# Preparing the value products of a hybrid decoder block: scale roots spread earlier, the first tile loaded whole, twelve warm-up matmuls

## The chip, the cores and the metric

The kernel runs on one core of a Trainium2 chip. The metric is the device time of one execution, in microseconds (us). TensorE (PE) multiplies, VectorE (DVE) and ScalarE (ACT) do the elementwise work, GpSimd (POOL) here only takes powers, and SyncE (SP) issues the transfers between the chip's memory and the on-chip buffers, one after another from one queue.

## The reference, cut to what matters

```
xn = rmsnorm(x, norm1_g)                         # x: 1024 tokens x 1024 channels
qa, ka, va, qr, kr, vr, gr, gate_a, gate_b = pieces of xn @ w_in
qa, ka = per-head rmsnorm
o_a = three groups of dilated sliding-window attention, mixed by their denominators
o_r = retention(qr, kr, vr), per-head groupnorm, times silu(gr)
y = sigmoid(gate_a) * (o_a @ w_proj_a) + sigmoid(gate_b) * (o_r @ w_proj_b)
x = x + y @ w_out
x = x + square(relu(rmsnorm(x, norm2_g) @ w_up)) @ w_down
```

All tensors are float32. The change touches only the first stage: the norm of `x` and `va`, the 1024 x 1536 values of attention, three column blocks of 512.

## The kernel before, in words

**Splits.** Each operand of a product is kept as two tensors, a rounded one (`xh`, `wh`, written by ScalarE) and the rest (`xl`, `wl`, by VectorE); `split` writes both (lines 401 and 404). A product is three matmuls for each 128 channels, xh.wh, xh.wl, xl.wh (line 297).

**Weights.** `W` streams the weights: `load` issues a transfer on SP, `pump` works through a list of steps (splits, and additions of weight quarters, line 157) as far as `W.limit` lets it, `hold` bounds the loads. `request(n)` raises `hold`, `weight_sums(n)` raises `limit`.

**The values.** The 1024 tokens are 8 tiles of 128. Column block 0 is done plainly: `columns(t)`, 24 matmuls. Blocks 1 and 2 for all tokens are done as a 2 x 2 block product with seven instead of eight products: N1 (`first_part`) and N2 (`second_part`) for tiles 0 to 3, 12 matmuls each, then N6, N5, N7, N3, N4, four tiles of 12 each, whose operands are sums of pieces of the normalised input (`sums`, line 734, then `put_sum`, which splits them). `keep_part`, `add_parts` and `keep_columns` move results out of the accumulators and `store` them.

**The norm.** `x` arrives twice: transposed (`load_k(t)`, operand layout) and in rows (`load_x(t)`). `root(t)` squares and sums the rows on ScalarE, takes the power on GpSimd, and writes a diagonal matrix of the roots on VectorE (line 634). `spread(t)` is a matmul of ones with that diagonal (line 646), which lays the roots along the free dimension. `times_root(t)` multiplies by them on VectorE, for a tile in `FUSED` by the norm weights at the same time (eight instructions, line 658), else in two instructions (line 661) after `times_g(t)` has done the norm weights on ScalarE (eight instructions, line 639). `put(t)` splits the result into the operand `X`. Tiles 0 and 1 (`RAWS`) are first multiplied without their roots (`raw_split`, lines 623 and 624), and the root is applied to the results.

**Order.** A call of a part emits its matmuls as one slot; `with_spread(t, fn)` puts a spread inside the slot of `fn`, behind half of a part's matmuls, or behind 9 of 24 in `columns`. In this stage ScalarE and VectorE run the instructions of the listed calls in the order in which they are emitted; work emitted outside the two `manual_schedule` blocks (the split of the weights of N5 and later, for instance) is placed among them by the scheduler of the framework, and so are SP's transfers. Matmuls of ones on a scratch operand (line 683) run ahead of the first product.

Of the kernel before, what the change touches and what calls it, by code (L numbers as in the profile page):

```python
# [19 lines left out]
D = 1024  # L20
# [17 lines left out]
class Weights:  # L38
# [10 lines left out]
    A, B, C, D = (0, 1), (2, 3), 5, 4  # L49
# [298 lines left out]
def hybrid_block(ctx: ExitStack, tc: tile.TileContext, a: dict, out: bass.AP):  # L348
    nc = tc.nc
# [76 lines left out]
    W = Weights(nc, rawp, wp, split)  # L426
# [165 lines left out]
    px = pool(first, "px", 2, "right")  # L592

    RAWS = 2
    FUSED = (2, 3, 0)
    ones = maskT[:, 0]
    busy = XS[0, 1][0][:, 0]
    col = gng.rearrange("p a b -> p (a b)")[:, :3 * NT].rearrange("p (t c) -> p t c", c=3)
# [4 lines left out]
    parts = [tuple(x[t // 2][:, t % 2 * 512:t % 2 * 512 + 512] for x in (half_a, half_e)) for t in range(4)]  # L603
    xk, xts = {}, {}

    def load_k(t, cut=slice(0, D)):

        to = half_e[t % 6] if t in (0, 1, 6) else px.tile([P, D], F, name="xk")
        xk[t] = to.rearrange("p (k t) -> p k t", k=KT)
        nc.sync.dma_start(to[:, cut], a["x_t"][t][:, cut])  # L610

    def load_x(t):
        xts[t] = px.tile([P, D], F, name="xt") if t else half_a[1]
        nc.sync.dma_start(xts[t], a["x"][t * P:(t + 1) * P, :])
# [14 lines left out]
    def root(t):  # L629

        nc.scalar.activation(xts[t], xts[t], AF.Square, accum_out=col[:, t, 0:1])
        rsqrt(col[:, t, 1:2], col[:, t, 0:1], 1.0 / D)
        dg[t] = FX[1, t // 4][:, 3, t % 4 * P:t % 4 * P + P]
        nc.vector.tensor_scalar(dg[t], ident, col[:, t, 1:2], None, op0=OP.mult)

    def times_g(t, ks=range(KT)):

        for k in ks:
            nc.scalar.activation(xk[t][:, k], xk[t][:, k], AF.Copy, scale=gT[:, k:k + 1])
# [11 lines left out]
    def times_root(t):  # L651

        pt = roots[t]
        for j in range(2):
            to = rooted(t, j)
            if t in FUSED:
                for k in range(4):
                    nc.vector.scalar_tensor_tensor(to[:, k], xk[t][:, 4 * j + k], gT[:, 4 * j + k:4 * j + k + 1],
                                                   pt[:, 0], op0=OP.mult, op1=OP.mult)
            else:  # L660
                nc.vector.tensor_tensor(to, xk[t][:, 4 * j:4 * j + 4], pt[:, 0:1].to_broadcast([P, 4, P]),
                                        op=OP.mult)

    def put(t):

        for j in range(2):
            split(*X(slice(4 * j, 4 * j + 4), tokens_of(t)), rooted(t, j))

    lo, hi = halves()
    with tc.manual_schedule(engines={mybir.EngineType.DVE, mybir.EngineType.Activation}):  # L670
        nc.sync.dma_start(gT, a["norm1_g"])
        load_k(0, slice(0, 512))
        W.limit = W.hold = 8
        W.load()
        load_k(0, slice(512, D))
        for _ in range(5):
            W.load()
        nc.vector.memset(busy.bitcast(F), 1.0)
        nc.vector.memset(ones, 1.0)
        nc.scalar.activation(col[:, 0, 2:3], half[:, 0:1], AF.Square)  # L680
        warm = mm.tile([P, 512], F, name="mm")
        for _ in range(9):
            nc.tensor.matmul(warm, busy[:, :P], busy, start=True, stop=True)
        raw_split(0, range(4))
        W.pump(1)
        raw_split(0, range(4, 6))
        W.pump(1)
        raw_split(0, range(6, 8))
        for _ in range(6):
            W.pump(1)  # L690
        load_k(1)
        load_x(0)
        nc.sync.dma_start(ident, a["c_ident"])
        load_k(2)
        load_x(2)
        load_x(1)
        load_k(3)
        raw_split(1, range(8))
# [29 lines left out]
    def sums(h, names):  # L728

        cut = slice(256 * h, 256 * h + 256)  # L730
        for name in names:
            t, u, op = {"N5": ((0, 0), (0, 1), OP.subtract), "N7": ((0, 1), (1, 1), OP.subtract),
                        "N6": ((1, 1), (0, 0), OP.add), "N4": ((1, 0), (1, 1), OP.subtract)}[name]
            nc.vector.tensor_tensor(FX[t][:, :, cut], FX[t][:, :, cut], FX[u][:, :, cut], op=op)

    def put_sum(name, h):

        cut = slice(256 * h, 256 * h + 256)
        split(*(x[:, :, cut] for x in operands[name]), FX[sums_of[name]][:, :, cut])
# [3 lines left out]

    nc.sync.dma_start(gqk[:, 0], a["q_norm_g"])
    nc.sync.dma_start(gqk[:, 1], a["k_norm_g"])
    SUM = {16: ("N5", 0), 17: ("N5", 1), 18: ("N7", 0), 19: ("N7", 1), 28: ("N4", 0), 29: ("N4", 1)}
    us, plain = W.take(4), W.take(4)
    made = {}
    raw = [t < RAWS for t in range(NT)]
# [1 line left out]
    def first_part(t):  # L751
        made["N1", t] = unit_part("N1", t, us[:2], ms, "ms")

    def second_part(t):
        made["N2", t] = unit_part("N2", t, us[2:], mm, "mm")

    def columns(t):
        made["P", t] = values(plain, tokens_of(t), t == NT - 1, ms, "ms")

    def keep_part(t):  # L760
        nc.scalar.activation(parts[t][0], made.pop(("N1", t)), AF.Copy, **({"scale": col[:, t, 1:2]} if raw[t] else {}))

    def add_parts(t):

        pm, vt = made.pop(("N2", t)), vp.tile([P, 512], F, name="vt")
        if raw[t]:
            nc.vector.scalar_tensor_tensor(vt, pm, col[:, t, 1:2], parts[t][0], op0=OP.mult, op1=OP.add)
        else:
            nc.vector.tensor_tensor(vt, pm, parts[t][0], op=OP.add)
        store(1, t, vt)  # L770

    def keep_columns(t):

        vt = vp.tile([P, 512], F, name="vt")
        nc.scalar.activation(vt, made.pop(("P", t)), AF.Copy, **({"scale": col[:, t, 1:2]} if raw[t] else {}))
        store(0, t, vt)

    def weight_sums(n):
        W.limit += n
        W.pump()  # L780

    def request(n):

        W.hold += n
        while W.load():
            pass

    def with_spread(t, fn):
        pipe.at(0, lambda: spread(t), lambda: None)
        fn()  # L790

    def open_sums():

        first.close()
        for name in ("N6", "N5"):
            open_slot(name)

    def save():
        for i, x in enumerate(XS[0, 1]):
            nc.sync.dma_start(xs_d[i], x.bitcast(F).rearrange("p a b -> p (a b)"))  # L800

    with tc.manual_schedule(engines={mybir.EngineType.DVE, mybir.EngineType.Activation}):
        first_part(0)
        second_part(0)
        columns(0)

        first_part(1)
        root(0)

        second_part(1)  # L810
        root(2)
        load_x(3)
        keep_part(0)
        add_parts(0)
        keep_columns(0)

        with_spread(2, lambda: columns(1))
        times_root(2)
        root(1)
        put(2)  # L820
        load_k(4)
        load_x(4)
        keep_part(1)
        add_parts(1)
        request(3)

        first_part(2)
        keep_columns(1)
        root(3)
        load_x(5)  # L830

        with_spread(3, lambda: second_part(2))
        times_root(3)
        load_k(5)
        times_g(4)

        with_spread(0, lambda: columns(2))
        keep_part(2)
        put(3)
        add_parts(2)  # L840
        times_root(0)
        load_k(6)
        root(4)
        load_x(6)
        put(0)
        weight_sums(2)
        request(3)

        with_spread(4, lambda: first_part(3))
        keep_columns(2)  # L850
        times_root(4)
        load_k(7)
        root(5)
        load_x(7)
        times_g(1, range(4))

        second_part(3)
        put(4)
        times_g(1, range(4, 8))
        weight_sums(1)  # L860

        with_spread(1, lambda: columns(3))
        keep_part(3)
        add_parts(3)
        times_root(1)
        put(1)
        weight_sums(2)
        times_g(5)
        root(6)

        with_spread(5, lambda: columns(4))
        keep_columns(3)
        times_root(5)
        put(5)
        weight_sums(1)
        times_g(6)
        sums(0, ("N5",))

        with_spread(6, lambda: columns(5))
        keep_columns(4)  # L880
        times_root(6)
        put(6)
        root(7)
        sums(0, ("N7", "N6"))
        times_g(7)

        with_spread(7, lambda: columns(6))
        keep_columns(5)
        times_root(7)
        put(7)  # L890
        open_sums()
        put_sum("N6", 0)
        weight_sums(2)

        columns(7)
        keep_columns(6)
        save()
        sums(1, ("N5", "N7", "N6"))
        put_sum("N6", 1)

    W.limit, W.hold = None, 18
    nc.vector.tensor_scalar(gqk[:, 0], gqk[:, 0], -DH ** -0.5, None, op0=OP.mult)
# [1 line left out]
    def front_step():  # L904
# [10 lines left out]
        if p == 28:  # L915
# [5 lines left out]
            open_slot("N4")  # L921
        if p in SUM:
            put_sum(*SUM[p])

# [183 lines left out]
    with ExitStack() as ph:  # L1108
# [6 lines left out]
        sums, squares = {}, {}  # L1115
# [281 lines left out]
    with ExitStack() as ph:  # L1397
# [115 lines left out]
        for i, (j, name) in enumerate(order):  # L1513
# [8 lines left out]
            if (j, name) in free:  # L1522
                u = free[j, name]
                lo, _ = halves()
# [121 lines left out]
    with ExitStack() as ph:  # L1646
# [56 lines left out]
        sums = {}  # L1703
# [126 lines left out]
    with ExitStack() as ph:  # L1830
# [5 lines left out]
        for u in range(1, len(units)):  # L1836
# [3 lines left out]
            c, t = units[u]  # L1840
# [112 lines left out]
```

## Time and profile before

| | us |
|---|---|
| median of 3 runs | 2156.54 (2155.95 to 2158.1) |
| the profiled execution, its time | 2162.37 |
| its span, first to last instruction | 2160.6 |
| first product (tile 0) starts | 6.41 |
| `first_part(1)` starts | 21.63 |
| `columns(7)` starts | 73.04 |
| N5 starts | 92.43 |

The profile shows one execution. TensorE is recorded busy 99% of the span; a matmul's record overlaps the next one's, so the distance of two starts tells more than a duration. The granted clock is the share of TensorE's full clock, 1.00 or less. In rows of the timeline the bracket names how long the engine had been idle, and who released it.

### The profile page before, as it was taken

The page shows a single profiled execution, that of the slowest core. Times are in us where ns is not written, and L with a number is a line of the kernel's source. Part 1 is how long each engine was busy: PE and PEld are TensorE (multiplying, and loading weights), DVE is VectorE, ACT ScalarE, POOL GpSimd, SP SyncE. Part 2 cuts the span into 40 slices and gives each one's busy share as a digit, 9 for nine tenths or more (in the row PEclk, how much of TensorE's full clock was granted, in tenths as well). Part 3 has the DMA queues.
Part 4 walks back from the last instruction along what each step waited for, and adds up shares of the span by engine and source line. Part 5 has one row for each costly group of instructions (what it writes and reads, how often), then busy time and mean ns, then how long its engine had stood idle before and what let it go on. Part 6 is the DMA issues. An engine that isn't in the chain of part 4 may idle for free.

```text
span 2160.6 us, 28517 instructions
## 1 busy us (share of the span) xinstructions
PE 2137.2 (99%) x9837; PEld 1751.6 (81%) x9837; DVE 1383.6 (64%) x2370; ACT 1110.5 (51%) x2125; POOL 311.1 (14%) x340
## 2 busy tenths in 40 slices
PE   9999999999999999999999999999999999999999
PEld 7787777788888888888888877778788888788887
DVE  6944434655556565657767776783865556788884
ACT  6625555434655454445545654542655555755552
POOL 0000000000000000003123110000000000777773
PEclk9999999999999999999999999999999999999999
DMA  8433333243667666665354587874254556745443
GB/s 317 153 106 113 103 96 114 99 138 132 189 202 217 205 197 195 214 182 168 107 173 129 160 288 237 273 235 147 87 161 143 160 156 195 237 157 186 161 141 108
DMA packets 296481, 366.15 MB, mean 169 GB/s; under 512 B 35136, under 2 KB 202496, under 8 KB 296080
## 3 DMA queue, kind: packets, MB, share of 16 engines
q1 hardware_dynamic: 295792, 364.06, 53.4%
q8 instruction: 77, 1.26, 0.2%
q14 instruction: 68, 0.56, 0.1%
q10 hardware_dynamic: 544, 0.26, 0.0%
HBM read 247.67 MB, written 116.59 MB: 169 GB/s over the span
## 4 chain that ended last, share of the span: by engine, by line
PE 81%; DVE 5%; DMA 5%; issue 3%; ACT 2%; POOL 1%; SPq 0%; POOLq 0%; DVEq 0%; ACTq 0%
PE mm L297 44%; PE ms L297 32%; PE tr L999 1%; PE tr L978 1%; DMA xl<-on_d 1%; DVE wl L404 1%; DVE xl L404 1%; DMA s<-sg_d 1%; DMA rb<-rs_d 1%; PE tr L989 1%; PE tr L1346 1%; DMA raw<-in_w_rv 1%; PE tr L1131 1%; PE ms L1286 1%; ACT wh L401 1%
## 5 line engine op out<-in xcount | busy, mean ns | idle before, releaser
L404 DVE TENSOR_TENSOR wl<-raw,wh 128x1024 fp32r<-128x1024 f32 (+1 forms) x313 | 347.0, 1110 | 408.0 <-ACT wh L401 406.9
L401 ACT ACTIVATE wh<-raw 128x1024 fp32r<-128x1024 f32 (+1 forms) x313 | 299.8, 961 | 296.7 <-PE ms L297 93.1
L297 PE MATMUL mm<-xh,wh 128*128 128x512 f32 x960 | 388.0, 404 | 3.2 <-ACT ms L474 2.5
L297 PE MATMUL mm<-xh,wl 128*128 128x512 f32 x960 | 375.0, 391 | 0.5 <-DVE wl L404 0.5
L297 PE MATMUL mm<-xl,wh 128*128 128x512 f32 x960 | 374.2, 390 | 0.9 <-DVE xl L404 0.9
L297 PE MATMUL ms<-xh,wh 128*128 128x512 f32 x784 | 318.0, 406 | 3.8 <-ACT u L482 2.1
L297 PE MATMUL ms<-xh,wl 128*128 128x512 f32 x784 | 306.2, 391 | 0.5 <-DVE wl L404 0.5
L297 PE MATMUL ms<-xl,wh 128*128 128x512 f32 x784 | 305.5, 390 | 0.0
L297 PEld LDWEIGHTS mm<-xh,wl 128*128 128x128 f32 x960 | 180.2, 188 | 40.3 <-DVE wl L404 1.4
L297 PEld LDWEIGHTS mm<-xh,wh 128*128 128x128 f32 x960 | 180.4, 188 | 39.1 <-ACT ms L474 3.3
L297 PEld LDWEIGHTS mm<-xl,wh 128*128 128x128 f32 x960 | 180.7, 188 | 35.3 <-DVE xl L404 1.3
L297 PE MATMUL mm<-wh,xh 128*128 128x512 f32 x514 | 208.4, 405 | 0.0
L297 PE MATMUL mm<-wh,xl 128*128 128x512 f32 x514 | 201.5, 392 | 0.0
L297 PE MATMUL mm<-wl,xh 128*128 128x512 f32 x514 | 200.7, 390 | 0.0
L297 PEld LDWEIGHTS ms<-xh,wh 128*128 128x128 f32 x784 | 147.4, 188 | 44.1 <-issue 10.1
L1319 POOL TENSOR_TENSOR st<-st,half 128x1 f32<-128x1 f32 x32 | 25.3, 790 | 1032.5 <-PE ms L297 874.5
L297 PEld LDWEIGHTS ms<-xh,wl 128*128 128x128 f32 x784 | 147.1, 188 | 32.8 <-DVE wl L404 1.0
L297 PEld LDWEIGHTS ms<-xl,wh 128*128 128x128 f32 x784 | 147.6, 188 | 27.0
L297 PEld LDWEIGHTS mm<-wh,xl 128*128 128x128 f32 x514 | 96.7, 188 | 21.6
L297 PEld LDWEIGHTS mm<-wh,xh 128*128 128x128 f32 x514 | 97.1, 189 | 18.3 <-ACT ms L1763 0.6
L297 PEld LDWEIGHTS mm<-wl,xh 128*128 128x128 f32 x514 | 97.2, 189 | 17.8
L129 DVE TENSOR_TENSOR raw<-raw,raw 128x512 f32<-128x512 f32 x120 | 83.6, 697 | 3.0
(344 smaller groups left out, 3728.5 us busy)
## 6 DMA issues: line engine op xcount, KB each, us to landing
raw<-in_w_up SPq DMA_DIRECT2D x32, 512.0 KB
h_d<-s SPq DMA_DIRECT2D x64, 256.0 KB
raw<-in_w_down SPq DMA_DIRECT2D x32, 512.0 KB
xl<-on_d SPq DMA_DIRECT2D x28, 512.0 KB
raw<-in_w_aqk_q SPq DMA_DIRECT2D x24, 512.0 KB
qk_d<-sg SPq DMA_DIRECT2D x48, 256.0 KB
qk<-qk_d SPq DMA_DIRECT2D x24, 512.0 KB
rb<-rs_d SPq DMA_DIRECT2D x24, 512.0 KB
```

The costliest lines, as they stand in the source:

```text
L129: ins = self.nc.vector.tensor_tensor(x, x, y, op=OP.add)
L297: self.nc.tensor.matmul(ps, x, y, start=start, stop=stop, skip_group_check=not first)
L401: hi = nc.scalar.activation(dst_h, src, AF.Copy)
L404: lo = nc.vector.tensor_tensor(dst_l, src, dst_h.bitcast(F), op=OP.subtract)
L978: nc.tensor.matmul(sp[:, to], q, qk[c][:, 1, (n0 - 4 * c) * P:(n1 - 4 * c) * P], start=True, stop=True)
L989: nc.tensor.transpose(tp[:, j], st["p"][:, j * P:(j + 1) * P], ident)
L999: nc.tensor.matmul(po, st["t"][:, j], V[k // 2][:, k % 2], start=(j == 0), stop=(j == nk - 1))
L1131: nc.tensor.matmul(to[m:m + 32], pick[:, 31 - n:63 - n], x, start=n == 0, stop=n == HEADS - 1)
L1286: nc.tensor.matmul(sp[:, :P], kT[:, f], qT[:, f], start=(f == 0), stop=(f == 1))
L1319: nc.gpsimd.tensor_tensor(st[:, 9:10], st[:, 8:9], half[:, 0:1], op=OP.pow)
L1346: nc.tensor.transpose(pt[:, f, :], it["o"][:, f * P:(f + 1) * P], ident)
```

## The change

Three edits, all in the first stage. (a) The first transposed tile is loaded in one transfer instead of two halves, ahead of the norm weights, which were first. (b) Twelve instead of nine matmuls of ones. (c) The order of the listed calls: the roots and spreads of most tiles, and the work behind them, move relative to the slots; tile 3 leaves `FUSED`; the first half of N5's sum splits, and the second, move from the slots of N6's first tiles to behind `columns(7)`; N6's second half moves ahead of `columns(7)`; `times_g(1)` is in one piece; the requests for weights and the additions of weight quarters move.

```diff
@@ -592,7 +592,7 @@
     px = pool(first, "px", 2, "right")
 
     RAWS = 2
-    FUSED = (2, 3, 0)
+    FUSED = (2, 0)
     ones = maskT[:, 0]
     busy = XS[0, 1][0][:, 0]
     col = gng.rearrange("p a b -> p (a b)")[:, :3 * NT].rearrange("p (t c) -> p t c", c=3)
@@ -603,11 +603,11 @@
     parts = [tuple(x[t // 2][:, t % 2 * 512:t % 2 * 512 + 512] for x in (half_a, half_e)) for t in range(4)]
     xk, xts = {}, {}
 
-    def load_k(t, cut=slice(0, D)):
+    def load_k(t):
 
         to = half_e[t % 6] if t in (0, 1, 6) else px.tile([P, D], F, name="xk")
         xk[t] = to.rearrange("p (k t) -> p k t", k=KT)
-        nc.sync.dma_start(to[:, cut], a["x_t"][t][:, cut])
+        nc.sync.dma_start(to, a["x_t"][t])
 
     def load_x(t):
         xts[t] = px.tile([P, D], F, name="xt") if t else half_a[1]
@@ -668,18 +668,16 @@
 
     lo, hi = halves()
     with tc.manual_schedule(engines={mybir.EngineType.DVE, mybir.EngineType.Activation}):
+        load_k(0)
         nc.sync.dma_start(gT, a["norm1_g"])
-        load_k(0, slice(0, 512))
         W.limit = W.hold = 8
-        W.load()
-        load_k(0, slice(512, D))
-        for _ in range(5):
+        for _ in range(6):
             W.load()
         nc.vector.memset(busy.bitcast(F), 1.0)
         nc.vector.memset(ones, 1.0)
         nc.scalar.activation(col[:, 0, 2:3], half[:, 0:1], AF.Square)
         warm = mm.tile([P, 512], F, name="mm")
-        for _ in range(9):
+        for _ in range(12):
             nc.tensor.matmul(warm, busy[:, :P], busy, start=True, stop=True)
         raw_split(0, range(4))
         W.pump(1)
@@ -743,7 +741,7 @@
 
     nc.sync.dma_start(gqk[:, 0], a["q_norm_g"])
     nc.sync.dma_start(gqk[:, 1], a["k_norm_g"])
-    SUM = {16: ("N5", 0), 17: ("N5", 1), 18: ("N7", 0), 19: ("N7", 1), 28: ("N4", 0), 29: ("N4", 1)}
+    SUM = {18: ("N7", 0), 19: ("N7", 1), 28: ("N4", 0), 29: ("N4", 1)}
     us, plain = W.take(4), W.take(4)
     made = {}
     raw = [t < RAWS for t in range(NT)]
@@ -806,97 +804,100 @@
 
         first_part(1)
         root(0)
-
-        second_part(1)
         root(2)
         load_x(3)
+
+        with_spread(2, lambda: second_part(1))
         keep_part(0)
         add_parts(0)
+        times_root(2)
         keep_columns(0)
-
-        with_spread(2, lambda: columns(1))
-        times_root(2)
         root(1)
         put(2)
         load_k(4)
         load_x(4)
+
+        columns(1)
+        times_g(3)
         keep_part(1)
         add_parts(1)
-        request(3)
-
-        first_part(2)
-        keep_columns(1)
         root(3)
         load_x(5)
-
-        with_spread(3, lambda: second_part(2))
+        request(3)
+
+        with_spread(3, lambda: first_part(2))
+        keep_columns(1)
         times_root(3)
+        put(3)
         load_k(5)
-        times_g(4)
-
-        with_spread(0, lambda: columns(2))
-        keep_part(2)
-        put(3)
-        add_parts(2)
-        times_root(0)
-        load_k(6)
+
+        with_spread(0, lambda: second_part(2))
         root(4)
         load_x(6)
+        times_root(0)
+        times_g(4)
         put(0)
+        load_k(6)
+
+        with_spread(4, lambda: columns(2))
+        keep_part(2)
+        add_parts(2)
+        times_root(4)
+        put(4)
+        load_k(7)
         weight_sums(2)
-        request(3)
-
-        with_spread(4, lambda: first_part(3))
-        keep_columns(2)
-        times_root(4)
-        load_k(7)
+        times_g(1)
         root(5)
         load_x(7)
-        times_g(1, range(4))
+        request(3)
+
+        with_spread(1, lambda: first_part(3))
+        keep_columns(2)
+        times_root(1)
+        put(1)
+        weight_sums(1)
 
         second_part(3)
-        put(4)
-        times_g(1, range(4, 8))
-        weight_sums(1)
-
-        with_spread(1, lambda: columns(3))
+        times_g(5)
+        root(6)
+        weight_sums(2)
+
+        with_spread(5, lambda: columns(3))
         keep_part(3)
         add_parts(3)
-        times_root(1)
-        put(1)
-        weight_sums(2)
-        times_g(5)
-        root(6)
-
-        with_spread(5, lambda: columns(4))
-        keep_columns(3)
         times_root(5)
         put(5)
+        times_g(6)
+        root(7)
         weight_sums(1)
-        times_g(6)
         sums(0, ("N5",))
 
-        with_spread(6, lambda: columns(5))
-        keep_columns(4)
+        with_spread(6, lambda: columns(4))
+        keep_columns(3)
         times_root(6)
         put(6)
-        root(7)
+        times_g(7)
         sums(0, ("N7", "N6"))
-        times_g(7)
-
-        with_spread(7, lambda: columns(6))
-        keep_columns(5)
+        weight_sums(1)
+
+        with_spread(7, lambda: columns(5))
+        keep_columns(4)
         times_root(7)
         put(7)
+        weight_sums(1)
+        sums(1, ("N5", "N7", "N6"))
+
+        columns(6)
+        keep_columns(5)
         open_sums()
         put_sum("N6", 0)
-        weight_sums(2)
+        put_sum("N6", 1)
+        save()
 
         columns(7)
         keep_columns(6)
-        save()
-        sums(1, ("N5", "N7", "N6"))
-        put_sum("N6", 1)
+        put_sum("N5", 0)
+        put_sum("N5", 1)
 
     W.limit, W.hold = None, 18
     nc.vector.tensor_scalar(gqk[:, 0], gqk[:, 0], -DH ** -0.5, None, op0=OP.mult)
```

## The prediction

> **What bounds the kernel now.** I read the head of the page first, then the matmuls of line 297 (all products) counted by stretch, with the chain of waits for the rate of one.
>
> ```profile
> span 2160.6 us, 28517 instructions
> PE 2137.2 (99%) x9837; PEld 1751.6 (81%) x9837; DVE 1383.6 (64%) x2370; ACT 1110.5 (51%) x2125; POOL 311.1 (14%) x340
> ...
> 6.41:21.63 15.22, 14.72 (x48) 10.91 (x49) 0.78 1.01 405
> 21.63:73.04 51.41, 51.41 (x218) 39.81 (x216) 1.00 0.60 216
> 73.04:92.43 19.39, 17.25 (x73) 13.28 (x72) 1.00 0.70 245
> 92.43:133.39 40.96, 40.96 (x182) 33.94 (x181) 1.00 0.33 116
> ...
> 133.39 13.60 PE mm L297 x60
> ```
>
> TensorE is the bound, and its busy share hides what is lost: matmuls are recorded overlapped. The chain gives 13.60/60 = 0.2267 us each. A part (`first_part`, `second_part`, one tile of N6) has 12 of them, 2.72 us; `columns` has 24, 5.44 us. The counts include one or two that straddle an edge; by the code the stretches hold 48, 216 with eight spreads, 72 and 180. So the opening (three slots of tile 0) has 15.22 - 48 x 0.2267 = 4.3 us of loss; the middle 51.41 - 48.97 = 2.4 us, nearly all of it the eight spreads; the tail (`columns(7)` and N6) 19.39 - 16.32 = 3.1 us; from N5 on there is none. Some 7.7 us is all that this stage can give, 0.36% of the time. Next I read the clock, and the timelines of the opening and of the tail.
>
> ```profile
> 7.50:8.00 0.50, 0.50 (x3) 0.43 (x2) 0.50 (x3) 0.00 (x0) 0.00 (x0) 0.80 0.94 385
> 8.00:14.50 6.50, 6.24 (x14) 4.10 (x14) 5.30 (x9) 5.47 (x9) 0.00 (x0) 0.50 1.03 413
> 14.50:15.00 0.50, 0.50 (x3) 0.43 (x2) 0.43 (x2) 0.37 (x1) 0.00 (x0) 0.88 1.05 426
> ...
> 0.74 0.39 SPq L671 DMA_DIRECT2D g<-in_norm_g  x1
> 1.19 0.41 SPq L610 DMA_DIRECT2D E<-in_x_t  x1
> 1.64 0.43 SPq L235 DMA_DIRECT2D raw<-in_w_av  x1
> 4.22 1.28 ACT L623 ACTIVATE xh<-E,g 128x128 fp32r<-128x128 f32 x4 [1.99 <-DMA E<-in_x_t]
> 5.73 1.15 ACT L401 ACTIVATE e0h<-raw 128x512 fp32r<-128x512 f32 x2 [0.23 <-DMA raw<-in_w_av]
> 6.41 0.50 PE L297 MATMUL ms<-e0h,xh 128*128 128x512 f32 x1 [1.25 <-ACT e0h L401]
> 8.68 1.15 ACT L401 ACTIVATE e1h<-raw 128x512 fp32r<-128x512 f32 x2 [1.21 <-DMA raw<-in_w_av]
> 11.07 7.60 DVE L404 TENSOR_TENSOR wl<-raw,wh 128x512 fp32r<-128x512 f32 x7
> ...
> 74.20 0.50 PE L297 MATMUL ms<-wh,xl 128*128 128x512 f32 x1 [0.54 <-DVE xl L404]
> 87.29 0.50 PE L297 MATMUL ms<-wh,xl 128*128 128x512 f32 x1 [1.08 <-DVE xl L404]
> ...
> 78.07 1.22 DVE L734 TENSOR_TENSOR fx<-fx 128x1024 f32<-128x1024 f32 x1
> 79.20 1.22 DVE L404 TENSOR_TENSOR wl<-raw,wh 128x1024 fp32r<-128x1024 f32 x1
> 80.34 1.22 DVE L734 TENSOR_TENSOR fx<-fx 128x1024 f32<-128x1024 f32 x1
> 81.47 1.22 DVE L404 TENSOR_TENSOR wl<-raw,wh 128x1024 fp32r<-128x1024 f32 x1
> 83.75 2.35 DVE L404 TENSOR_TENSOR wl<-raw,wh 128x1024 fp32r<-128x1024 f32 x2
> 86.02 2.35 DVE L404 TENSOR_TENSOR xl<-fx,xh 128x1024 fp32r<-128x1024 f32 x2
> ```
>
> In the opening the granted clock is 0.50 from 8 to 14.5 us. In the tail VectorE is the late one: `columns(7)` waits for the split of tile 7, and the third tile of N6 for the split of the second half of N6's sum, behind the sums (L734) and four weight roundings (L404 `wl`) that stand between them in VectorE's queue. It starts at 87.29 less two matmuls already issued, 86.84. That is my mark: what the change does to this start is what it does to the time, since nothing is lost behind it.
>
> **The opening.** The issues are 0.45 apart. The first tile is asked for at 0.74 instead of 1.19 and one request is gone, so all bytes flow 0.45 earlier; the tile is whole, 256 KB more (0.63 us at the 413 GB/s above) ahead of the first weights. First weights: 5.73 + 0.63 - 0.45 = 5.91, so the first product at 6.6 instead of 6.41. From the second weights on the bytes ahead are the same: 8.68 becomes 8.23, the last one's rounding 11.07 + 7.60 = 18.67 becomes 18.22. The norm weights (4 KB) land behind the tile that needs them anyway: no cost while they share its queue; at worst one more transfer's lag, 0.45. Three more matmuls of ones take 0.68 at full clock inside the 1.25 us idle ahead of 6.41; without that cover they would cost 0.68.
>
> What they may buy is the clock. With the last weights at 18.22 and five matmuls behind them, `first_part(1)` cannot start before 18.22 + 1.13 = 19.4 (case A, the clock back early); with the same half-clock stretch it starts some 0.3 before the old 21.63, at 21.3 (case B). I hold them equal: the idle between the ones and the first product shrinks only from 1.25 (by the recorded end) to about 0.8, but the halt ahead of 8.68 shrinks too. The Trainium skill ("TensorE: Matmul & The Clock Gate", Part 1) says that the gate closes after an idle window of some 3.4 us; the trace disagrees, since the clock halved after 1.25 us of idling at most. By that rule alone three more matmuls of ones change nothing in the clock, and case B stands.
>
> **The middle: root, spread, times_root, put.** These rows price one tile's loop.
>
> ```profile
> 21.70 1.06 ACT L631 ACTIVATE xt<-xt 128x1024 f32<-128x1024 f32 x1 [0.57 <-DMA xt<-in_x]
> 23.70 0.29 DVE L634 TENSOR_SCALAR fx<-ident,gng 128x128 f32<-128x128 f32 x1 [0.67 <-POOL gng L420]
> 29.11 0.38 PE L646 MATMUL tr<-fx,maskT 128*128 128x128 f32 x2
> 29.53 2.16 DVE L658 SCALAR_TENSOR_TENSOR fx<-xk,g,tr 128x128 f32<-128x128 f32 x8 [4.80 <-PE tr L646]
> 53.45 1.27 DVE L661 TENSOR_TENSOR fx<-E,tr 128x512 f32<-128x512 f32 x2
> 54.16 1.23 ACT L401 ACTIVATE xh<-fx 128x512 fp32r<-128x512 f32 x2 [2.26 <-DVE fx L661]
> 54.83 1.29 DVE L404 TENSOR_TENSOR xl<-fx,xh 128x512 fp32r<-128x512 f32 x2
> 55.30 2.44 ACT L639 ACTIVATE xk<-xk,g 128x128 f32<-128x128 f32 x8
> 56.04 2.48 DVE L157 TENSOR_TENSOR raw<-raw,raw 128x1024 f32<-128x1024 f32 x2
> 57.65 1.04 ACT L631 ACTIVATE xt<-xt 128x1024 f32<-128x1024 f32 x1
> ```
>
> `root` takes 23.99 - 21.70 = 2.3 from the square to the diagonal, 1.04 of it on ScalarE; spread to scaling 0.42; unfused scaling and `put` 56.04 - 53.45 = 2.59 of VectorE, with ScalarE released 1.85 after the start; fused scaling 2.07; `times_g` 2.35 of ScalarE; one addition or sum 1.14 of VectorE; `keep_part` or `keep_columns` 0.6.
>
> Tile 3 leaves FUSED: VectorE is spared 2.07 - 1.20 = 0.9, ScalarE gets 2.35 more, beside matmuls in both. The count of spreads stays at eight. Let T be the start of the scaling of tile 2: either 4.5 behind `first_part(1)` (its spread now lies 18 matmuls behind that start), or behind the root of tile 2 (the square at 21.70 - 0.45, plus 2.3) and one addition of 0.6, 24.15. In case A T is 24.15, in B 25.8; before it was 29.53. If no wait fell, N6's third tile would start at T + 57.4 (4.5 before T, then 264 matmuls at 0.2267 and eight spreads of about 0.25: 61.9).
>
> The new order makes each pass serial: ScalarE does `times_g` and then the square, VectorE waits for that root before it scales the next tile, ScalarE waits for the scaling. From `columns(2)` a pass is 0.72 + 1.13 (scaling to the end of the two roundings) + 2.35 + 2.2 = 6.4 us, against a `columns` slot of 5.44 + 0.25 = 5.7. Following the emission order: diagonal 3 at T + 7.9 (PE reaches its spread at T + 8.0), 4 at 12.5 (14.6), 5 at 22.9 (26.0), 6 at 29.3 (31.7), 7 at 38.7 (37.4). So seven of the spreads are ready, the last with its margin gone: in `columns(5)` TensorE waits 1.3 us on the diagonal of tile 7, while VectorE idles 2.8 us for `times_g(6)` and the square. Behind that: two sums, scaling and `put(6)`, two sums, N6's first weight rounding, then `put(7)`, whose first xl is ready at T + 49.3 where `columns(7)` wants it at 48.35: 1.0. Then N6's second weight rounding, three sums and the xl of N6's first half, ready at T + 56.0, wanted at 54.8: 1.2. The second half follows at 57.2, before its use. Together 3.5: N6's third tile starts at T + 60.9.
>
> The splits of N5 move ahead of N6's tiles but behind N6's own: 2 x 1.14 beside 10.9 us of N6, hidden. On SP the second `request(3)` goes behind `load_x(7)`, thus behind the square of tile 5 (T + 21.7); four transfers of 512 KB at 413 GB/s plus the 3.0 us from issue (1.19) to use (4.22) end at T + 30, and the two additions that need them run at T + 29.2 to 31.6, the last row at about 30.4: no cost, 0.5 at worst. Earlier, `load_x(3)` passes nothing that waits.
>
> **Sum.** Case A: 24.15 + 60.9 = 85.05, 1.8 us gained. Case B: 86.7, 0.1 gained. Unknown is where the weight roundings of N5 and N7 go, which are outside the hand-written order: four stood between sums before (79.20 to 83.75), 1.14 each in front of the split TensorE waits for. None to four may now stand ahead of N6's first split: 0 to 4.55. I take none (6 in 10) or one, since the sums are now a slot earlier and the weights' buffers still come free in `columns(7)`: mean 0.9 gained with none, 0.2 lost with one, so 0.45 gained. The profiled execution is 2162.37 at a span of 2160.6, the runs' median 2156.54; I take the difference from the median: 2156.1.
>
> **Rivals.** (1) The passes are quicker than I lay them and VectorE never keeps TensorE waiting: 2.2 of the opening and all 3.1 of the tail come back, 5.3, 2151.2. For it: VectorE scales tile 2 some 4 us earlier and is spared 0.9. Against: the 6.4 us pass, and the last weights at 18.22. It counts as faster only if 4.3 of the 5.3 are there. (2) Slower: all four weight roundings land ahead of N6's first split in a case B opening: 86.7 + 4.55 = 91.3, 4.4 later, 2161.0. Decisive from the fourth on. For it: the pattern at 79.20 to 83.75; against: the buffers. (3) The opening gains, and gives it all back: the wait moves from N6's third tile to the last spread and N6's first tile, 2156.5; that is the edge of my own case.
>
> **Chances.** A measurement here tells 0.2%, 4.3 us, from no change. My case with (3), within that: 0.83; rival 1 beyond it: 0.10; rival 2: 0.07. My case alone runs from 2154.2 (A, none) to 2159.2 (B, two), with half a us for the runs' spread; the range reaches down towards rival 1 and up to B with three: 2152.3 to 2159.8.
>
> **What would show it.** The opening: granted clock after 8 us, and the start of `first_part(1)` (19.4 or 21.3). The middle: scaling of tile 2 at 24 to 26; an idle stretch of VectorE of over 2 us ahead of the root of tile 7, and TensorE halted ahead of the spread in `columns(5)`. The tail: the L404 rows that stand between the sums and N6's first xl; N6's third tile at 85 to 88. I am wrong if TensorE runs from `first_part(1)` to N5 with under 1 us lost, or if a weight load comes late on SP's queue and VectorE's additions wait for it.

## The result, and the profile after

The changed kernel takes 2162.59 us (median of 14 runs, 2158.64 to 2165.34) where the kernel before, run beside it, takes 2157.44 (14 runs, 2153.95 to 2161.81): a ratio of 1.002 [1.0012, 1.0028]. In a second comparison, later, it was 2162.16 against 2159.37, 1.0012 [1.0004, 1.0021]. It is slower, by 2.8 to 5.2 us, where 0.4 us of gain was predicted. The changed kernel gave nearly the same median twice; the median of the kernel before moved by 1.9 us between the two.

The two profiled executions hide this. The head of the page after:

```profile
span 2160.8 us, 28527 instructions
PE 2140.0 (99%) x9840; PEld 1754.4 (81%) x9840; DVE 1384.2 (64%) x2364; ACT 1111.9 (51%) x2133; POOL 312.0 (14%) x340
```

Its span is 0.2 us over that of before, because the profiled execution of before (2162.37) lay above all 14 runs of its comparison, 4.9 us over their median. The stages tell more. The matmuls of line 297 after the change, by stretch (stretch, its length, busy TensorE and weight loads with counts, granted clock, DMA share, GB/s): opening, middle, `columns(7)` with N6, and the 192 matmuls behind.

```profile
6.77:19.66 12.89, 12.47 (x49) 9.06 (x49) 1.00 1.03 409
19.66:73.92 54.26, 51.39 (x217) 39.72 (x215) 1.00 0.61 212
73.92:94.71 20.79, 18.65 (x72) 14.61 (x73) 0.92 0.67 241
94.71:138.23 43.52, 43.52 (x193) 36.05 (x192) 1.00 0.33 115
```

The opening is 2.0 us shorter at its end (19.66 for 21.63), at full clock from 7.7 us on. The middle is 2.85 longer (54.26 for 51.41), the tail 1.4 longer (20.79 for 19.39) at a clock of 0.92. N5 starts 2.3 later. From there on no loss: 43.52/192 = 0.2267 for each matmul.

Where TensorE waited, by the view of the waits from 18 to 95 us (total, times, longest):

```profile
PE ms L297 <- DVE xl L404: 2.1, 1, 2.1
PE ms L297 <- ACT xh L401: 1.4, 1, 1.4
PE tr L646 <- DVE fx L634: 1.2, 1, 1.2
```

and in its timeline:

```profile
63.11 0.46 PE L646 MATMUL tr<-fx,maskT 128*128 128x128 f32 x2 [1.25 <-DVE fx L634]
73.92 0.50 PE L297 MATMUL ms<-wh,xh 128*128 128x512 f32 x1 [1.36 <-ACT xh L401]
82.53 0.61 PE L297 MATMUL ms<-wh,xl 128*128 128x512 f32 x1 [2.14 <-DVE xl L404]
```

These are the three places that the prediction named: ahead of the last spread, of `columns(7)` and in N6's first tile. By distance of starts, less 0.2267, the halts lose 1.41, 1.53 and 2.30 us, 5.2 together. The matmul that ends the third takes 0.61, where the one that ends the second takes 0.50. That is the clock, which the stretches ahead of 82.80 and behind it show (columns as above):

```profile
79.39:82.80 3.41, 1.27 (x6) 0.77 (x5) 1.00 0.67 244
82.80:86.20 3.40, 3.40 (x9) 2.62 (x9) 0.50 0.64 202
```

For 3.4 us TensorE got half its clock: some 1.6 us lost again, which no halt shows. VectorE's and ScalarE's timelines give the reasons of the halts:

```profile
24.16 2.16 DVE L658 SCALAR_TENSOR_TENSOR fx<-xk,g,tr 128x128 f32<-128x128 f32 x8 [0.27 <-PE tr L646]
58.35 2.44 ACT L639 ACTIVATE E<-E,g 128x128 f32<-128x128 f32 x8
60.69 1.04 ACT L631 ACTIVATE xt<-xt 128x1024 f32<-128x1024 f32 x1
61.86 0.15 DVE L419 TENSOR_SCALAR gng<-gng 128x1 f32<-128x1 f32 x1 [2.69 <-ACT xt L631]
...
67.74 3.73 DVE L732 TENSOR_TENSOR fx<-fx 128x1024 f32<-128x1024 f32 x3
71.39 1.22 DVE L404 TENSOR_TENSOR wl<-raw,wh 128x1024 fp32r<-128x1024 f32 x1
72.53 1.28 DVE L661 TENSOR_TENSOR fx<-xk,tr 128x512 f32<-128x512 f32 x2
...
75.45 1.23 DVE L404 TENSOR_TENSOR wl<-raw,wh 128x1024 fp32r<-128x1024 f32 x1 [0.25 <-ACT wh L401]
76.59 2.48 DVE L732 TENSOR_TENSOR fx<-fx 128x1024 f32<-128x1024 f32 x2
78.99 1.22 DVE L404 TENSOR_TENSOR wl<-raw,wh 128x1024 fp32r<-128x1024 f32 x1
80.12 1.22 DVE L732 TENSOR_TENSOR fx<-fx 128x1024 f32<-128x1024 f32 x1
81.26 1.22 DVE L404 TENSOR_TENSOR xl<-fx,xh 128x1024 fp32r<-128x1024 f32 x1
```

ScalarE does `times_g(6)` (58.35) ahead of the square of tile 7 (60.69), and VectorE idles 2.69 us for it: the first halt. Three sums instead of two (67.74) and a weight rounding stand ahead of the scaling of tile 7 (72.53): the second. Two more weight roundings (75.45, 78.99) stand among the sums ahead of N6's first `xl` (81.26): the third.

### The profile page after: what moved, and what is told of

Same layout as the page of the kernel before. It is cut to its first block, busy times and chain, and to the rows that moved or that the text cites. A ratio compares the mean times of both kernels' runs of the same rounds, so it can differ in the third digit from the quotient of the medians.

```text
span 2160.8 us, 28527 instructions
## 1 busy us (share of the span) xinstructions
PE 2140.0 (99%) x9840; PEld 1754.4 (81%) x9840; DVE 1384.2 (64%) x2364; ACT 1111.9 (51%) x2133; POOL 312.0 (14%) x340
## 4 chain that ended last, share of the span: by engine, by line
PE 81%; DVE 6%; DMA 3%; issue 3%; ACT 2%; POOL 2%; SPq 0%; POOLq 0%; DVEq 0%; ACTq 0%
PE mm L297 43%; PE ms L297 32%; PE tr L1000 1%; PE tr L979 1%; DVE wl L404 1%; DVE xl L404 1%; PE tr L990 1%; DVE raw L129 1%; DMA s<-sg_d 1%; ACT xh L401 1%; PE tr L1132 1%; PE tr L1347 1%; DMA xl<-on_d 0%; ACT wh L401 0%; PE ms L1287 0%
```

## The experiments

Experiments 1 to 4, 5 to 8 and 9 to 12 are three groups, on three chips, and all kernels of a group ran beside the kernel before. "Pinned" means that the splits of weights stay where the listing of calls emits them (experiment 7). The stretch is the time from the start of `first_part(1)` to that of N5 in one trace; it leaves the opening out. All twelve, with the halts in that stretch in order (spread of tile 7, `columns(7)`, N6):

| kernel | median, before's median | ratio | `first_part(1)` | stretch | halts |
|---|---|---|---|---|---|
| before (as predicted from) | | | 21.63 | 70.80 | 0, 0.71, 0.68 + 1.25 |
| after | 2162.59, 2157.44 | 1.002 [1.0012, 1.0028] | 19.66 | 75.05 | 1.41, 1.53, 2.30 |
| before again | 2159.19, 2159.49 | 1.0 [0.999, 1.0009] | 20.03 | 70.74 | as before |
| opening only | 2157.83, 2159.49 | 0.9997 [0.9988, 1.0006] | 19.57 | 70.75 | as before |
| order only | 2161.37, 2159.49 | 1.0013 [1.0004, 1.0022] | 20.27 | 73.45 | 1.40, 1.53, 2.31 |
| after, halt filled | 2162.52, 2159.49 | 1.0015 [1.0004, 1.0025] | 20.14 | 73.46 | 1.41, 1.51, filled |
| after, root 7 first | 2159.28, 2159.42 | 1.0 [0.999, 1.001] | 20.11 | 72.73 | 0, 0.77, 2.31 |
| after, N6's sum first | 2160.66, 2159.42 | 1.0006 [0.9995, 1.0016] | 19.97 | 72.43 | 1.40, 1.51, 1.27 |
| mended, pinned | 2156.64, 2159.42 | 0.9985 [0.9975, 0.9996] | 19.80 | 68.28 | 0, 0, 0.67 |
| before, pinned | 2157.9, 2159.42 | 0.9992 [0.9982, 1.0001] | 20.23 | 70.21 | 0, 0.68, 1.21 |
| after again | 2162.16, 2159.37 | 1.0012 [1.0004, 1.0021] | 22.44 | 75.06 | 1.42, 1.53, 2.29 |
| after, pinned | 2160.03, 2159.37 | 1.0007 [0.9998, 1.0016] | 20.86 | 72.42 | 1.41, 1.56, 1.29 |
| mended, not pinned | 2160.92, 2159.37 | 1.0008 [0.9999, 1.0017] | 20.08 | 71.39 | 0, 0, 0.85 + 1.27 |
| mended, pinned, old opening | 2154.56, 2159.37 | 0.998 [0.9971, 0.9988] | 20.31 | 68.28 | 0, 0, 0.68 |

**1. The kernel before once more**, for its own spread in the stages.

> The kernel before, once more. Theory 1 (the gate): whether TensorE's clock halves in the opening depends on the execution, so the profile of before that the prediction rested on is one draw. Then the mean granted clock varies from run to run between 1.000 and 0.997, the runs at 1.000 are the quick ones, and in a trace without the half-clock stretch first_part(1) starts near 20 us instead of 21.6 and N5 near 91 instead of 92.4. Theory 2 (VectorE's queue alone): the half-clock stretch from 7.5 to 14.5 us is there in every execution, all runs show 0.998 and first_part(1) starts at 21.6 again.

```profile
6.39:20.03 13.64, 12.51 (x49) 8.88 (x49) 1.00 1.02 407
20.03:71.42 51.39, 51.39 (x218) 39.81 (x217) 1.00 0.63 227
71.42:90.77 19.35, 17.19 (x74) 13.28 (x72) 1.00 0.68 245
```

The same kernel, with the old order of transfers and nine matmuls of ones, starts `first_part(1)` at 20.03, not 21.63, and has a clock of 1.00 from its first product on. The half clock of 7.8 to 14.6 us, from which the prediction drew 2.2 us to be had, belonged to that execution. Middle and tail repeat within 0.04 us.

**2. The opening alone** (before, with the whole first tile, the norm weights behind it, twelve matmuls of ones).

```diff
...
+        load_k(0)
         nc.sync.dma_start(gT, a["norm1_g"])
-        load_k(0, slice(0, 512))
...
-        for _ in range(9):
+        for _ in range(12):
```

> Before with the two edits of the opening alone (first tile whole and ahead of the norm weights, twelve matmuls of ones). Theory 1: first_part(1) starts at 19.7, but most runs of before start it early too, so the time is 0 to 1 us under before, ratio 0.9995 to 1.0. Theory 2: 1.9 us gained in every run, carried to N5 (90.5 instead of 92.4), ratio 0.999.

```profile
6.57:19.57 13.00, 12.27 (x48) 8.88 (x49) 1.00 1.03 407
```

The first product starts 0.18 later (6.57 for 6.39, 0.2 was worked out), `first_part(1)` 0.46 earlier; the ratio of 0.9997 [0.9988, 1.0006] does not tell it from no change.

**3. The order alone** (after, with the old opening: experiment 2's diff taken back).

> The changed kernel with the opening of before (split tile behind the norm weights, nine matmuls of ones): the new order alone. Both theories: TensorE halts ahead of the spread of tile 7 (1.3 us), ahead of columns(7) (1.4) and in N6's first tile (2.1). Theory 1: about as slow as the changed kernel, 4 to 5 us over before, ratio 1.002. Theory 2: the opening's 2 us are missing as well, 6 to 7 us over before, ratio 1.003.

```profile
83.16 0.50 PE L297 MATMUL ms<-wh,xl 128*128 128x512 f32 x1 [2.15 <-DVE xl L404]
```

The stretch behind that halt (busy time of all five engines, clock, DMA):

```profile
83.00:86.10 3.10, 2.94 (x13) 2.44 (x14) 3.10 (x4) 3.10 (x6) 0.00 (x0) 1.00 0.65 215
```

The loss is here: 1.0013 [1.0004, 1.0022], with a median under what either theory expected (1.002, 1.003), with the same three halts, and a stretch 2.7 us longer than that of before (73.45 for 70.74). But behind the halt the clock stays at 1.00, so the stretch is 1.6 shorter than after's. Halts and the clock are two costs.

**4. The halt filled**: ten matmuls on scratch data ahead of N6's first tile, beside the whole change.

```diff
+            if name == "N6" and t == 0:
+                fill = tr.tile([P, 512], F, name="tr")
+                x = XS[0, 0][0][:, 0]
+                for _ in range(10):
+                    nc.tensor.matmul(fill, x[:, :P], x, start=True, stop=True)
```

> The changed kernel with ten matmuls into a scratch bank between columns(7) and N6's first tile, where TensorE halts for 2.1 us: 2.3 us of filling that needs nothing. Theory 1: the halt is as long as before, but the granted clock stays at 1.00 behind it, N6's first tile takes 2.7 us from its third matmul on instead of 3.9, N5 starts at 93.0 to 93.3 instead of 94.7, and the time is 1.5 us under the changed kernel. Theory 2: the clock in N6 is not what is lost; N5 starts at 94.7 or later.

```profile
80.30 2.43 PE L938 MATMUL tr<-xh 128*128 128x512 f32 x10
```

```profile
83.00:86.10 3.10, 3.10 (x14) 2.55 (x14) 3.10 (x3) 3.10 (x5) 0.00 (x0) 1.00 0.62 200
```

N6's first tile waits as long, but TensorE is busy meanwhile and the clock stays at 1.00: the stretch is that of the order alone (73.46) and 1.6 below after's. In the times the 1.5 us expected cannot be seen (1.0015); the half clock is not in every execution, as experiment 3 shows. Nor does this one trace show that it was the filling that kept the clock, since the halt falls here as it does in experiment 3 (last section); what speaks for it is that 1 of 11 runs has a mean clock of 0.998 or less, against 12 of 25 of after.

**5. The square of tile 7 ahead of `times_g(6)`.**

```diff
-        times_g(6)
         root(7)
+        times_g(6)
```

> The changed kernel with root(7) emitted ahead of times_g(6) instead of behind it; nothing else. Measure: the time from the start of first_part(1) to the start of N5, 70.7 to 70.8 in three traces of the old order, 73.5 in two of the new one, and 75.05 in the third, where the clock halved in N6. Theory 1 (one serial chain of root, times_g and scaling through VectorE and ScalarE sets all three halts): the diagonal of tile 7 is ready 2.3 us earlier, TensorE does not halt ahead of its spread, columns(7) waits some 0.7 us instead of 1.5, N6's first tile still about 2; the stretch takes 71.2. Theory 2 (VectorE's work ahead of N6's first split is what counts, and the idle time ahead of root 7 is made up elsewhere): the halt only moves into N6, 73.5 as before.

```profile
59.97 0.15 DVE L419 TENSOR_SCALAR gng<-gng 128x1 f32<-128x1 f32 x1 [0.34 <-ACT xt L631]
...
80.66 0.50 PE L297 MATMUL ms<-wh,xl 128*128 128x512 f32 x1 [2.15 <-DVE xl L404]
```

VectorE's idle time ahead of root 7 falls from 2.69 to 0.34, the first halt goes, the second halves. N6's halt stays and brings half a clock again (from 81.2, 3.4 us). Without that, 72.73 - 1.7 = 71.0. Two calls in the other order on ScalarE are worth 2.3 us of stretch, and the ratio is 1.0.

**6. N6's first half sum and its split straight behind `put(7)`.**

```diff
         put(7)
+        open_sums()
+        put_sum("N6", 0)
         weight_sums(1)
         sums(1, ("N5", "N7", "N6"))
...
-        open_sums()
-        put_sum("N6", 0)
         put_sum("N6", 1)
```

> The changed kernel with the split of N6's first half emitted right behind put(7), ahead of the addition, the second weight rounding and the three sums of the second half. Theory 1: the halts ahead of the spread of tile 7 (1.3 us) and of columns(7) (1.5) stay, the one in N6's first tile (2.1) goes, and a smaller one, under 1 us, comes ahead of N6's third tile, where the second half is late; the stretch takes 71.5 to 72. Theory 2: N6's first tile waits for other things as well (its weights), 73 or more.

```profile
PE ms L297 <- DVE xl L404: 1.1, 1, 1.1
```

The halt of 2.3 goes from N6's first tile, and 1.27 comes back in its third, as in the kernel before: four weight roundings stand ahead of that tile's split now. One microsecond of 2.3 is gained, and no half clock follows in this trace.

**7. Both mended, and the weight splits pinned.** The square of tile 7 first; N6's sums one slot later and its first split next behind them; and the splits of weights kept where the listing emits them.

```diff
...
-                self.split(*hl, self.raw[r])
+                self.split(*hl, self.raw[r], True, True)
...
-        times_g(6)
         root(7)
+        times_g(6)
...
-        sums(0, ("N7", "N6"))
-        weight_sums(1)
+        sums(0, ("N7",))
...
         put(7)
-        weight_sums(1)
+        sums(0, ("N6",))
+        open_sums()
+        put_sum("N6", 0)
+        weight_sums(2)
         sums(1, ("N5", "N7", "N6"))
...
-        open_sums()
-        put_sum("N6", 0)
         put_sum("N6", 1)
```

> The changed kernel with the queue of VectorE and ScalarE mended in three places: root(7) ahead of times_g(6); put(7) ahead of the N6 sum of the first half and of the roundings of N6's weights, and N6's first split right behind them; the splits of the value weights kept in the order of emission, so that none of N5's and N7's is placed ahead of N6's splits. Theory 1: no halt of TensorE over 0.5 us from first_part(1) to N5; the stretch takes 68.0 to 68.6, N5 starts near 88, and the kernel is 2.5 to 3 us under before, ratio 0.9987. Theory 2: one of the halts stays, 70 or more, ratio 1.0.

```profile
71.88 1.22 DVE L404 TENSOR_TENSOR xl<-fx,xh 128x1024 fp32r<-128x1024 f32 x1
81.68 3.49 DVE L404 TENSOR_TENSOR xl<-fx,xh 128x1024 fp32r<-128x1024 f32 x3
85.09 4.63 DVE L404 TENSOR_TENSOR wl<-raw,wh 128x1024 fp32r<-128x1024 f32 x4
...
82.95 0.50 PE L297 MATMUL ms<-wh,xl 128*128 128x512 f32 x1 [0.50 <-DVE xl L404]
```

The four weight roundings stand behind the sums' splits (85.09 behind 81.68), N6's first `xl` is there at 71.88, far ahead of N6, and one halt of 0.67 is left. The stretch is 68.28, 2.5 below that of before, and the time is below it: 0.9985 [0.9975, 0.9996].

**8. The pin alone, on the kernel before** (the first two changed lines of the diff above).

> The kernel before with only the splits of the value weights kept in the order of emission, so that the four weight roundings of N5 and N7 do not stand between the sums and N6's second split in VectorE's queue. Theory 1: the halt ahead of N6's third tile (0.5 and 1.1 us) goes, the one ahead of columns(7) stays; the stretch from first_part(1) to N5 takes 69.0 to 69.3 instead of 70.75, ratio 0.9993. Theory 2: the sums themselves are late, 70.5 or more.

```profile
82.31 0.69 DVE L935 TENSOR_TENSOR A<-ms,A 128x512 f32<-128x512 f32 x1
82.91 2.35 DVE L404 TENSOR_TENSOR xl<-fx,xh 128x1024 fp32r<-128x1024 f32 x2
```

```profile
PE ms L297 <- DVE xl L404: 1.6, 2, 1.0
```

A miss: 70.21 where 69.0 to 69.3, a larger gain, was expected. No weight rounding stands there any more, but the splits of N5's sum and an addition (82.31) took its place, and N6's third tile still waits 1.21.

**9. The whole change once more.**

> The changed kernel once more, on the chip of the next three. Theory 1 (order and gate): first_part(1) near 19.6 to 20.1, the same three halts (1.4, 1.5, 2.3 us), the stretch to N5 73.5 if the clock stays and 75 if the 2.3 us halt falls into one window of the gate; time 2.5 to 4.5 us over before, ratio 1.0012 to 1.002. Theory 2 (the first comparison was a drift of the chip): ratio 1.000.

```profile
7.63 1.15 ACT L401 ACTIVATE e0h<-raw 128x512 fp32r<-128x512 f32 x2 [1.85 <-DMA raw<-in_w_av]
8.31 0.79 PE L297 MATMUL ms<-e0h,xh 128*128 128x512 f32 x1 [2.47 <-ACT e0h L401]
...
8.00:14.50 6.50, 6.18 (x14) 4.58 (x15) 6.21 (x12) 6.38 (x13) 0.00 (x0) 0.50 1.02 414
86.30:89.70 3.40, 3.40 (x9) 2.64 (x9) 3.40 (x4) 3.40 (x5) 0.00 (x0) 0.50 0.73 259
```

The opening was expected to be quick and is not. The first weights are rounded at 7.63 instead of 6.08 in after, the first product starts at 8.31 with TensorE idle for 2.47 ahead of it, the clock is half from 8 to 14.5 us in spite of twelve matmuls of ones, and `first_part(1)` starts at 22.44. The tail repeats after's to 0.01 us, with the half clock behind the halt.

**10. The pin alone, on the change.**

> The changed kernel with only the splits of the value weights kept in the order of emission: no weight rounding of N5 stands ahead of N6's first split any more. Theory 1: that split is ready one rounding (1.14 us) earlier, the halt in N6's first tile is 1.2 instead of 2.3, the other two halts stay (1.4 and 1.5), the clock stays; the stretch from first_part(1) to N5 takes 72.3 against 73.5. Theory 2 (the three sums alone make it late): the halt stays at 2.3.

```profile
77.79 3.74 DVE L732 TENSOR_TENSOR fx<-fx 128x1024 f32<-128x1024 f32 x3
81.44 1.22 DVE L404 TENSOR_TENSOR xl<-fx,xh 128x1024 fp32r<-128x1024 f32 x1
...
82.72 0.50 PE L297 MATMUL ms<-wh,xl 128*128 128x512 f32 x1 [1.13 <-DVE xl L404]
```

The three sums and N6's first `xl` now stand together, and N6's halt is 1.29 instead of 2.30: one weight rounding is the difference. The clock stays at 1.00 there. In the opening TensorE idles 1.51 ahead of a late first product (7.75), and the clock is half from 8.7 to 12.1.

**11. The mended order without the pin.**

> The mended order without keeping the weight splits in the order of emission. Theory 1: the first two halts and the one in N6's first tile stay away, since they hang on the order of root, put and N6's first split; the four weight roundings come ahead of N6's second split and TensorE halts 2 to 3.5 us ahead of N6's third tile; the stretch takes 70 to 71.5 against 68.3. Theory 2: the order of emission of the weight splits made nothing; 68.3.

```profile
82.97 0.50 PE L297 MATMUL ms<-wh,xh 128*128 128x512 f32 x1 [0.68 <-ACT vt L773]
84.80 0.80 PE L297 MATMUL ms<-wh,xl 128*128 128x512 f32 x1 [1.10 <-DVE xl L404]
```

Two halts, 0.85 and 1.27, at N6's third tile, the first for ScalarE, which copies a result out of the accumulators late (L773), and the second for the split; then half a clock from 84.7: 71.39. Order and pin are both needed.

**12. Experiment 7 with the old opening.**

> The mended order with the weight splits kept in order, and with the opening of before (split first tile behind the norm weights, nine matmuls of ones). Theory 1: first_part(1) starts at 20.0 or, where the clock halves in the opening, 21.6, against 19.6 to 20.1 with the new opening; the stretch to N5 takes 68.3 all the same; ratio 0.9987 to 0.999. Theory 2 (the opening's edits carry the gain): ratio 1.000.

```profile
20.31:71.46 51.15, 51.10 (x218) 39.96 (x216) 1.00 0.66 235
71.46:88.59 17.13, 16.62 (x73) 13.41 (x72) 1.00 0.42 150
```

Middle and tail are those of experiment 7 to 0.01 us (68.28); the tail has 17.13 where before has 19.35. The time is 2154.56 against 2159.37, 0.998 [0.9971, 0.9988]: the fastest of all kernels here, 4.8 us below the one before, with none of the change's opening. The stretch accounts for 2.5 of them, and the same stretch gave 2.8 in experiment 7; no trace shows where the other 2 come from.

## Why the prediction was wrong, point by point

**The step that failed first: the opening's loss.** "So the opening ... has 4.3 us of loss" was read from one execution. Without a half clock past 11.1 us, the old opening starts `first_part(1)` at 20.03, 20.27, 20.23 and 20.31, the new one at 19.57 to 20.14 (seven traces, mean 19.90): 0.3 us is what the edits gain, not 2.2. With it, 21.63 (old), 22.44 and 20.86 (new, experiments 9 and 10). Both openings have shown cases A and B, but not from the same cause. In the new one the first weights are late: rounded at 5.75 to 7.63 in nine traces (5.91 was worked out), against 5.64 to 5.73 in five of the old one, so that the first product starts at 6.42 to 8.31 instead of 6.32 to 6.41. The two latest are experiments 10 and 9, where TensorE idles 1.51 and 2.47 ahead of it and the clock halves; what held the weights up there stays open. In before's trace the ones, at full clock from 4.4 on, were done early and left 1.25 us of idling.

The three more matmuls of ones were priced at full clock, 0.68, but all matmuls of ones start 0.43 apart until the clock rises: twelve take 5.49 us in after's trace and nine 3.67 in before's. Nor do they change nothing in the clock, as the prediction had it by the rule that it cites: with nine, TensorE has half the clock until 10.6 and 11.1 us in experiments 3 and 8 (matmuls 0.43 apart, though the column of the clock shows 1.00 until a trace's first change), while with twelve it has risen by 7.7 us in all nine traces. That gains nothing in the start of `first_part(1)`: 20.27 and 20.23 there, 20.03 and 20.31 where nine were enough. So the mean gain of the opening, which the sum used up against the tail, was not there. Rival 3 has its second half borne out (the wait did move to the last spread and N6's first tile), and not its first: there was no gain of the opening's to give back.

**The step that failed second: the size of the tail.** T was right (24.16, forecast 24.15 in case A). The serial pass, VectorE's idle time ahead of root 7 (2.69, forecast 2.8) and the three places were right. N6's third tile started at T + 65.1 (89.27) instead of T + 60.9. The 4.2 us between are: halts of 5.24 instead of 3.5, 1.7; the half clock behind the third, 1.6; and a base that was 0.9 too short (65.1 - 5.24 - 1.6 = 58.3, not 57.4). Of the 1.7, one weight rounding ahead of N6's first split accounts for 1.0 (experiment 10); this was named as unknown, and "none" was taken with 6 in 10. The second halt is longer by 0.5 with a third sum (1.14) in VectorE's queue ahead of the scaling of tile 7, which the listing does not put there: eight sums run where the listed calls make six, and the other two are those of N4, emitted outside the hand-written order. In before's trace the first of these stood behind that scaling (72.32 behind 71.13). The scheduler's freedom was priced for weight roundings, and not for sums.

**What was missing: the clock as a price of a halt.** No term of the sum held that a halt of 2.3 us can cost 1.6 us more behind its end; the clock was priced in the opening alone. Three of four traces with that halt have it (after, experiments 5 and 9; not 3), and after and 9 are 1.6 us longer for it than 3, with the same order. That filling the halt prevents it is likely and not shown (experiment 4).

**What was right.** The splits of N5's sum hidden beside N6; no late weights for VectorE's additions; nothing lost from N5 on. Rival 1's statement that the tail holds 3 us was right in itself: experiments 7 and 12 take 2.5 of them, with the order of two calls and the place of the splits. Rival 2 ended near the time, 2161.0, by another mechanism than it named: one rounding and not four.

**The sum now.** Opening 0.3 gained; order 2.7 lost (73.45 - 70.74); the half clock 1.6 lost in part of the executions, 1.2 with three in four: 3.6 us, between the 2.8 and 5.2 of the two comparisons. The times agree without any trace. Of the 101 runs of the kernel before in experiments 1 to 12, those with a mean granted clock of 1.000 have a median of 2157.7 (33 runs); those of after at that clock 2160.4 (3) and 2161.0 (2, experiment 9), of the order alone 2160.2 (3): 2.5 to 3.3 for the order at equal clock. And a mean clock of 0.998 or less came in 12 of 25 runs of after, 4 of 11 of the order alone, 25 of 101 of before, 2 of 11 with the halt shortened by the pin (experiment 10) and 1 of 11 with it filled.

**What stays open.** Behind N5, traces drift against each other by up to 2 us in both directions, also two of the same kernel: before starts N5 1.66 later than in experiment 1 but ends 3.2 later (spans of 2160.6 and 2157.4). Half a clock for 3.4 us near 1300 us, which executions of both orders have, is not the reason there: of these two traces it is in that of experiment 1, which ends earlier. The rest was not traced, and why the new opening's first weights come late in some executions was not either.

## What to carry to other kernels

Before a loss is put down as something to repair, see it in two executions: of the 7.7 us read in one profile, 1.3 to 1.6 were a draw (21.63 against 20.31 and 20.03). Where two engines pass a tile back and forth, look for the one instruction ahead of the awaited one on each queue (here `times_g` ahead of a square, a weight rounding ahead of a split): moving it gave more than moving whole slots earlier, and a hand-written order holds only for what is written in it. A halt of TensorE has to be priced with the clock behind it: here that cost 1.6 us more wherever the halt left less than 2 us of work in one step of 3.4.

## What the runs showed of the hardware that was not expected

The clock was halved behind stretches in which TensorE was not idle throughout: the 3.41 us ahead of 82.80 had it busy for 1.27 us (37%), and the clock came back after 3.4 us. The same halt in experiment 3 left it at 1.00. Half-clock stretches last 3.4 us or twice that, and in experiment 9 the end of the first (14.63) and the start of the second (86.31) lie 71.68 us apart, 21 times 3.413. So it is in all fourteen traces: by their records of the clock, all its changes in one trace lie whole multiples of 3.413 us apart, the longest over 600 of them. The clock is set at fixed steps, whose place in the program differs from run to run, and what counts is TensorE's work within one step. In experiment 3 the halt lies across two (columns as there):

```profile
78.89:82.31 3.42, 2.12 (x10) 1.43 (x8) 3.42 (x4) 2.79 (x4) 0.00 (x0) 1.00 0.81 273
82.31:85.72 3.41, 2.56 (x11) 2.13 (x12) 3.41 (x4) 3.41 (x5) 0.00 (x0) 1.00 0.60 222
```

Neither step is followed by half a clock; in after's trace and experiments 5 and 9 the halt leaves 1.27, 1.27 and 1.28 us of work in one step, and each is. Cut into such steps from its first change to 2150 us, every trace says the same: half a clock followed each of the 13 steps at full clock with 0.98 to 1.94 us of recorded TensorE work, and none of the 8756 with 2.01 or more. (Behind 2150 us, as the kernel ends, one step with 1.52, experiment 5's from 2153.1, is an exception.) In experiment 4 the third matmul of N6's first tile starts 0.09 us earlier within its step than in experiment 3, so without the filling some 2.03 us of work would have been left in the step, an estimate from 2.12: the clock would probably have stayed even so. The Trainium skill ("TensorE: Matmul & The Clock Gate", Part 1) states such a free-running window of 3413 ns, and these traces agree with its length; but it has the gate close after an idle window, and here one that was over half busy (1.94 of 3.41) was enough.

The price of the clock in a whole run: of the runs of the kernel before, a mean granted clock of 1.000 goes with 2157.7 us and one of 0.998 with 2161.6 (18 runs): 3.9 us, more than the 2.7 of the whole order.
